# PEER layer on one core: used experts found by VectorE from their products, the spare branch laid out the other way, zeros in one pass

## The chip, the cores and the metric

The kernel runs on one core of one Trainium2 chip. The metric is device time in microseconds (us) for one whole execution; the figure of a kernel is the median of several runs. One execution of the kernel before was also profiled, and all rows below are read from that profile. PE is the matmul engine, DVE the vector engine, ACT the scalar engine, POOL the GpSimd engine and SP the queue that issues most plain DMAs. PE's weight loads have a row of their own, PEld; the rows of an engine's sequencer (branches, waits) carry a q behind the name, as in PEldq.

## The reference, cut to what matters

One decoder layer on 256 tokens of width 2048: attention, then a product-key expert layer (PEER), then a gated embedding, each followed by a layer norm. The change lies in the expert layer. Each token picks 8 x 16 = 128 of 16384 experts, and each expert is one row of `u` and one row of `v`:

```
ub = u[eb]; vbk = v[eb]
act = gelu(einsum('the d,td->the', ub, xb))
w = gb * act
out = einsum('the,thed->td', w, vbk)
```

`eb` holds the expert numbers and `gb` the softmax gates. An expert number is `ia * 128 + ib`.

## The kernel before, in words

**Two ways for tokens.** The first 88 tokens (`NSP`) are done sparsely: POOL gathers their `u` and `v` rows into buffers `gb`, and DVE multiplies and sums them (L854, L864). For the other 168 tokens (`NDT`) the kernel computes all experts by matmul. The sparse work is spread over the dense stages, so many gathers for each dense block.

**Stage u.** `u_block(ia)` multiplies 128 experts of one `ia` with all dense tokens (L210, 32 PE records of 128x168 a block) and writes gelu of it into a table A0, A1 or A2 (one row for each `ib`, one column for each `ia` and token). Their weights `wf<-peer_u` are 1 MB for each block, in 5 buffers.

**Gates.** `gate_work` multiplies the tables with the gates, three tokens (`GB`) at a time. DVE compares with a row of numbers (L937, L939), ACT scales the one-hot rows into a high and a low half (L943, L944), PE multiplies (L951, L952: `ps_G`), and DVE multiplies the table in place (L968). It runs twice: for `ia` 0 to 67 (part 0) beside the u blocks 68 and after, and for `ia` 68 to 127 (part 1) beside the first v blocks. Each run has 56 groups of three tokens. The PE stream of part 0 is placed by the scheduler, the DVE stream by hand (`keep`).

**Counts.** Besides the two gate products there is a third for each token, of the unscaled one-hot rows: it counts how many times an expert was chosen. In part 0 it adds up all tokens in one PSUM bank that is held for it (`ps_cnt`, L954). In part 1 it adds up three tokens (L958) and DVE takes the maximum over groups (L974, L976).

**Lists.** `list_work` turns the counts into a list of used experts: a mask `m` (L1019), ranks by small matmuls, then the index tiles `idxV` and `idxW`. Part 0 lists up to 46 blocks of 128 used experts, part 1 up to 40 (`CAPS`).

**Stage v.** For each of the 86 listed blocks POOL gathers 128 rows of `v` (`vf`, 1 MB, 5 buffers) and of the stored tables (`wc`), and PE multiplies them into six PSUM banks (L1209, 32 records a block). The banks are first zeroed by a matmul (`v_bank`, L1216), with PE weights `ident` and data `zero` in float32.

**The branch.** If more experts are used than the lists hold, 42 more blocks follow (`rest`). This is decided at run time by `tc.If(more > 0)` (L1334), which each engine takes for itself. For this input the list holds all, so the 42 blocks are skipped. Behind the branch PE does the last three blocks (`held`) bank by bank, and then layer norm and the gated embedding.

Of the kernel before, what the change touches and what calls it, by code (L numbers as in the profile page):

```python
# [9 lines left out]
F32 = mybir.dt.float32  # L10
F32R = mybir.dt.float32r
F16 = mybir.dt.float16
U32 = mybir.dt.uint32
AF = mybir.ActivationFunctionType
ALU = mybir.AluOpType
AX = mybir.AxisListType
# [3 lines left out]
P = 128  # L20
T = 256
# [18 lines left out]
SEG1 = 68  # L40
# [3 lines left out]
PARTS = ((0, SEG1), (SEG1, SEG2))  # L44
# [5 lines left out]
NSP = sum(n for _, n in GROUPS)  # L50
# [10 lines left out]
GB = 3  # L61

EARLY, HEARLY = 5, 7
OHB = 4

STAG, LEAD, NWC = 3, 4, 8
NZERO = 3
# [91 lines left out]
def build(tc, a, out):  # L159
# [7 lines left out]
    def pbank(pool, name, tag="bank", bufs=4):  # L167
        return pool.tile([P, 512], F32, name=name, tag=tag, bufs=bufs)
# [450 lines left out]
    gin = pools.open("gin", "left", bufs=1)  # L619
    io128 = gin.tile([P, P], F16, name="io128")  # L620

    zero = gin.tile([P, 1], F32, name="zero")
    nc.gpsimd.memset(zero, 0.0)
    eig, eact, ew = [], [], []
    for i, (_, n) in enumerate(GROUPS):
# [187 lines left out]
    def gathers(n):  # L813

        nonlocal due
        due += n
        while due >= 1:
            due -= 1
            run(sparse, 1)
# [97 lines left out]
        keep(nc.tensor.matmul(ps[:, :nd * P], sel[2], ys[2][:, d0 * P:(d0 + nd) * P],  # L917
                              start=False, stop=False))

    def gate_work(oh, parts, s0, ns, group, counts, listed):  # L920

        def one_hot(t0, n):
            def rows(x, m):
                return x[:, None, :].to_broadcast([P, n, m])

            def cols(x, m):  # L930
                return x[:, t0:t0 + n, None].to_broadcast([P, n, m])

            ohb = oh.tile([P, group, P], F16, name="ohb", tag="ohb", bufs=OHB)
            eq = oh.tile([P, group, ns], F16, name="eq", tag="eq", bufs=OHB)
            hi = oh.tile([P, group, ns], F16, name="hi", tag="hi", bufs=OHB)
            lo = oh.tile([P, group, ns], F16, name="lo", tag="lo", bufs=OHB)
            keep(nc.vector.tensor_tensor(eq[:, :n], rows(io128[:, s0:s0 + ns], ns), cols(iaT, ns),  # L937
                                         op=ALU.is_equal))
            keep(nc.vector.tensor_tensor(ohb[:, :n], rows(io128, P), cols(ibT, P),  # L939
                                         op=ALU.is_equal))  # L940
            for j in range(n):
                t = slice(t0 + j, t0 + j + 1)
                nc.scalar.mul(hi[:, j, :], eq[:, j, :], ghf[:, t])  # L943
                nc.scalar.mul(lo[:, j, :], eq[:, j, :], glf[:, t])  # L944
            return ohb, eq, hi, lo

        def product(t0, n, ohb, eq, hi, lo):
            ps = pbank(pa, "ps_G")
            for j in range(n):
                o = ps[:, j * ns:(j + 1) * ns]  # L950
                nc.tensor.matmul(o, ohb[:, j, :], hi[:, j, :], start=True, stop=False)  # L951
                nc.tensor.matmul(o, ohb[:, j, :], lo[:, j, :], start=False, stop=True)  # L952
                if counts is not None:
                    nc.tensor.matmul(counts, ohb[:, j, :], eq[:, j, :], start=t0 + j == NSP,  # L954
                                     stop=t0 + j == T - 1)
            if counts is None:
                for j in range(n):
                    nc.tensor.matmul(ps[:, n * ns:(n + 1) * ns], ohb[:, j, :], eq[:, j, :],  # L958
                                     start=j == 0, stop=j == n - 1)
            return ps  # L960

        def scale(t0, n, ps):
            g = ps[:, :n * ns].rearrange("p (t a) -> p a t", t=n)
            c0 = 0
            for At in parts:
                dst = At[:, :, t0 - NSP:t0 - NSP + n]
                c1 = c0 + At.shape[1]
                keep(nc.vector.scalar_tensor_tensor(dst, g[:, c0:c1], 1.0 / GSCALE, dst,  # L968
                                                    op0=ALU.mult, op1=ALU.mult))
                c0 = c1  # L970
            if counts is None:
                new = ps[:, n * ns:(n + 1) * ns]
                if t0 == NSP:
                    keep(nc.vector.tensor_copy(total_cnt, new))  # L974
                else:
                    keep(nc.vector.tensor_tensor(total_cnt, total_cnt, new, op=ALU.max))  # L976

        total_cnt = counts
        if counts is None:
            total_cnt = oh.tile([P, ns], F32, name="cnts", tag="used2")  # L980
        made, multiplied = [], None
        for t0 in list(range(NSP, T, group)) + [None] * OHB:
            if t0 is not None:
                n = min(group, T - t0)
                made.append((t0, n, one_hot(t0, n)))
            if multiplied:
                scale(*multiplied)
                multiplied = None
            yield
            if made and (len(made) > OHB - 2 or t0 is None):  # L990
                m = made.pop(0)
                multiplied = (m[0], m[1], product(m[0], m[1], *m[2]))
                yield
        if multiplied:
            scale(*multiplied)
        yield from list_work(oh, parts, s0, ns, total_cnt, listed)

    idxV, idxW, over = [], [], []
    total = gin.tile([P, 1], mybir.dt.int32, name="total")

    def list_work(oh, parts, s0, ns, cnt, listed):


        part = len(idxV)
# [11 lines left out]

        store(2)
        m = oh.tile([P, ns], F16, name="m", tag="m")
        keep(nc.vector.tensor_scalar(m, cnt, 1.0, None, op0=ALU.min))  # L1019
        yield  # L1020
        store(1)

# [160 lines left out]
        return vf, wc  # L1183

    fetched = []
    cnt0 = pbank(pa, "ps_cnt")
    work = gate_work(ohp, (A0, A1), *PARTS[0], GB, cnt0[:, :SEG1], 6)
    for ia in range(SEG1, NIA):
        u_block(ia, W_of(ia))

        made = ia - SEG1
        if made < 38:
            run(work, 3)
        elif ia < NIA - 5:
            run(work, 1)
        elif ia == NIA - 5:
            while not run(work, 1):
                pass
            pools.close("a1p", "a0p")
            wcp = pools.open("wcp", "right", bufs=1)  # L1200
            work = gate_work(ohp, (A2,), *PARTS[1], GB, None, 3)
        if ia >= NIA - 4:
            fetched.append(v_fetch(*order.pop(0), sup, wcp, ("wf", "wc")))
        gathers(GUG if made < 38 else GUL)
# [8 lines left out]
    def v_bank(pool, n):  # L1213

        ps = pbank(pool, "ps_v")
        keep(nc.tensor.matmul(ps[:, :n], ident, zero.to_broadcast([P, n]),  # L1216
                              start=True, stop=False))
        return ps

# [104 lines left out]
    for b in range(LEAD + 1, N1 - STAG):  # L1324
        v_blocks(1, wcq)
        gathers(GV)
        if b == N1 - STAG - 1:
            while not run(sparse, 1):
                pass
# [1 line left out]
    natural_parts(ylp)  # L1331

    fbp = pools.open("fbp", "left", bufs=1)
    with tc.If(more > 0, preferred_fallthrough_block=False):  # L1334
        for i, b in rest:
            block = v_fetch(i, b, fbp, fbp, ("vf", "wc_"))
            for d in range(ND):
                v_mm(d, *block, False)
# [372 lines left out]
```

## Time and profile before

| | us |
|---|---|
| median of 3 runs | 1710.34 |
| lowest and highest run | 1708.72, 1712.31 |
| profiled execution | 1708.22 |
| its span in the trace | 1706.4 |
| PE busy | 1682.3 (99%) |
| DVE busy | 1098.9 (64%) |
| ACT busy | 556.1 (33%) |
| POOL busy | 609.5 (36%) |

The busy time of an engine is the union of its instructions. Matmuls overlap in PE, so their printed durations are longer than what one more of them costs: that is the distance between the starts of one and the next. HBM moved 325 GB/s over the span.

### The profile page before, as it was taken

What the parts mean: (1) busy time and instruction counts of PE and PEld (TensorE: products, weight loads), DVE (VectorE), ACT (ScalarE), POOL (GpSimd) and SP (SyncE); (2) the same over time, 40 slices, a digit from 0 to 9 for tenths busy, and PEclk for the clock granted to TensorE, in tenths of its full rate; (3) what the DMA queues carried; (4) which work ended last, traced back from release to release, by engine and by line L of the source; (5) the groups of instructions that cost most, each with busy time, mean ns of one, the idle gap of its engine ahead of it and who ended that gap; (6) DMA issues with size and microseconds to landing.
All of it is one profiled execution on the core that took longest, in us unless ns stands there. A gap on an engine that the chain in (4) does not pass through costs nothing. (4 is left out here: it accounts for less than half of the span.)

```text
span 1706.4 us, 29275 instructions
## 1 busy us (share of the span) xinstructions
PE 1682.3 (99%) x11258; PEld 1563.7 (92%) x11258; DVE 1098.9 (64%) x2290; ACT 556.1 (33%) x1396; POOL 609.5 (36%) x624
## 2 busy tenths in 40 slices
PE   9999999999999999999999999999999999998998
PEld 7888888888889999999999999999999999998886
DVE  5565489763589779844467765785776943333676
ACT  5677468753111100010044552005553000001452
POOL 0134023103345422722232322137554787673000
PEclk9999999999999999999999999999999999999999
DMA  7544644483998999999999999979999999997571
GB/s 294 195 155 162 234 160 156 156 323 133 338 419 327 390 421 417 419 420 421 421 415 405 371 384 392 422 293 394 392 383 382 418 412 415 401 396 281 187 269 50
DMA packets 97444, 555.63 MB, mean 326 GB/s; under 512 B 13366, under 2 KB 16966, under 8 KB 41846
## 3 DMA queue, kind: packets, MB, share of 16 engines
q0 software_dynamic: 43056, 285.38, 41.7%
q1 hardware_dynamic: 52086, 264.99, 40.3%
q10 hardware_dynamic: 2160, 3.34, 0.6%
q8 instruction: 92, 1.51, 0.3%
q14 instruction: 50, 0.41, 0.1%
HBM read 536.80 MB, written 17.04 MB: 325 GB/s over the span
## 5 line engine op out<-in xcount | busy, mean ns | idle before, releaser
L210 PE MATMUL ps_u<-XF,wf 128*128 128x168 f32 x3936 | 581.3, 308 | 7.5 <-DMA wf<-peer_u 7.1
L210 PEld LDWEIGHTS ps_u<-XF,wf 128*128 128x128 f32 x3936 | 562.5, 190 | 14.1 <-issue 11.8
L1209 PE MATMUL ps_v<-wc,vf 128*128 128x168 f32 x2752 | 414.8, 309 | 5.5 <-issue 5.5
L1209 PEld LDWEIGHTS ps_v<-wc,vf 128*128 128x128 f32 x2752 | 395.9, 191 | 7.3 <-issue 6.8
L120 DVE TENSOR_TENSOR wl<-wf,wh 128x1024 fp32r<-128x1024 f32 (+1 forms) x199 | 212.7, 1092 | 109.8 <-ACT wh L119 108.2
L854 DVE SCALAR_TENSOR_TENSOR gb<-gb,xq 128x2048 f32<-128x2048 f32 x88 | 203.4, 2316 | 99.0 <-DMA gb<-u_rows,eig 99.0
L864 DVE SCALAR_TENSOR_TENSOR y<-gb,ew,y 128x2048 f32<-128x2048 f32 x78 | 183.0, 2346 | 76.4 <-DMA gb<-v_rows,eig 76.3
L119 ACT CAST wh<-wf 128x1024 fp32r<-128x1024 f32 (+1 forms) x199 | 172.0, 892 | 121.0 <-PE ps_v L219 33.0
L1114 ACT ACTIVATE A<-ps_u 128x168 f32<-128x168 f32 x128 | 39.6, 310 | 459.7 <-PE ps_u L210 456.8
L198 PE MATMUL ps_qk<-X,wh 128*128 128x512 f32 x512 | 185.2, 401 | 0.0
L886 POOL DMA_INDIRECT gb<-u_rows,eig x88 | 94.6, 1075 | 246.6 <-DVE gb L854 151.4
L886 POOL DMA_INDIRECT gb<-v_rows,eig x88 | 104.3, 1185 | 132.6 <-DVE y L864 36.4
L200 PE MATMUL ps_qk<-X,wl 128*128 128x256 f32 x512 | 145.7, 285 | 0.0
L943 ACT ACTIVATE hi<-eq,ghf 128x68 f16<-128x68 f16 (+1 forms) x336 | 113.0, 336 | 87.4 <-DVE eq L937 87.3
L1180 POOL DMA_INDIRECT vf<-v_rows,idxV x86 | 107.2, 1246 | 83.9 <-PE ps_G L958 45.1
L1180 POOL DMA_INDIRECT wc<-s_w,idxW x86 | 102.9, 1197 | 40.4 <-issue 24.9
L198 PEld LDWEIGHTS ps_qk<-X,wh 128*128 128x128 f32 x512 | 96.4, 188 | 21.9 <-issue 1.0
L210 PE MATMUL ps_q<-XF,wf 128*128 128x256 f32 x512 | 113.5, 379 | 0.0
L944 ACT ACTIVATE lo<-eq,glf 128x68 f16<-128x68 f16 (+1 forms) x336 | 112.3, 334 | 0.0
L968 DVE SCALAR_TENSOR_TENSOR A<-ps_G,A 128x18 f32<-128x18 f32 (+2 forms) x168 | 46.9, 308 | 100.4 <-PE ps_G L958 44.0
L210 PEld LDWEIGHTS ps_q<-XF,wf 128*128 128x128 f32 x512 | 95.9, 190 | 12.3
L200 PEld LDWEIGHTS ps_qk<-X,wl 128*128 128x128 f32 x512 | 96.3, 188 | 2.5 <-issue 1.3
(309 smaller groups left out, 2127.2 us busy)
## 6 DMA issues: line engine op xcount, KB each, us to landing
wf<-peer_u SPq DMA_DIRECT2D x123, 1024.0 KB
wf<-w_qk SPq DMA_DIRECT2D x64, 512.0 KB
wf<-w_out SPq DMA_DIRECT2D x32, 512.0 KB
wf<-peer_wq SPq DMA_DIRECT2D x16, 1024.0 KB
wf<-ple_gate SPq DMA_DIRECT2D x16, 1024.0 KB
s_w<-A SPq DMA_DIRECT2D x14, 672.0 KB
wf<-w_v SPq DMA_DIRECT2D x16, 512.0 KB
wf<-w_sv SPq DMA_DIRECT2D x15, 512.0 KB
```

The source lines that it names most:

```text
L119: self.order(nc.scalar.copy(wh, src))
L120: self.order(nc.vector.tensor_tensor(wl, src, wh.bitcast(F32), op=ALU.subtract))
L198: nc.tensor.matmul(ps, wh[:, j * P:(j + 1) * P], xt[:, dt, :], start=dt == 0, stop=False)
L200: nc.tensor.matmul(ps[:, :T], wl[:, j * P:(j + 1) * P], xt[:, dt, :T], start=False, stop=dt == ND - 1)
L210: nc.tensor.matmul(ps[:, :T - t0], wf[:, dt * P:(dt + 1) * P], xt[:, dt, t0:], start=dt == 0, stop=dt == ND - 1)
L854: keep(nc.vector.scalar_tensor_tensor(g, g, 1.0, xq[i], op0=ALU.mult, op1=ALU.mult, accum_out=eact[i][:, j:j + 1]))
L864: keep(nc.vector.scalar_tensor_tensor(ys[i], g, ew[i][:, j:j + 1], ys[i], op0=ALU.mult, op1=ALU.add))
L886: keep(nc.gpsimd.indirect_dma_start(out=g, out_offset=None, in_=a[kind], in_offset=bass.IndirectOffsetOnAxis(ap=eig[i][:, 0, j:j + 1], axi ...
L943: nc.scalar.mul(hi[:, j, :], eq[:, j, :], ghf[:, t])
L944: nc.scalar.mul(lo[:, j, :], eq[:, j, :], glf[:, t])
L1180: keep(nc.gpsimd.indirect_dma_start(out=dst, out_offset=None, in_=src, in_offset=bass.IndirectOffsetOnAxis(ap=idx[:, b:b + 1], axis=0)))
L1209: return nc.tensor.matmul(psv[d // 3][:, d % 3 * NDT:(d % 3 + 1) * NDT], vf[:, d * P:(d + 1) * P], wc, start=False, stop=last and (d % 3 = ...
```

## The change

Three things are changed.

**Used experts.** The count products and their PSUM bank are gone. After each 24 tokens (`USED`) that have been scaled, DVE takes the largest absolute value of each expert's scaled products over these 24 tokens (`tensor_reduce` from the table in SBUF, one for A0 and one for A1 in part 0, one for A2 in part 1) and folds it into `greatest` with a maximum. There are 7 such turns in each part. The mask is now `greatest > 0`.

**The branch.** The skipped body now stands next in the program and the short other path behind it (`preferred_fallthrough_block=True`). A hint for PE is asked for two blocks ahead of the branch: it names the branch as likely taken.

**Zeros.** `v_bank` multiplies with `io128` and a `zero` that are both float16.

```diff
+USED = 24
-    zero = gin.tile([P, 1], F32, name="zero")
+    zero = gin.tile([P, 1], F16, name="zero")
...
-                if counts is not None:
-                    nc.tensor.matmul(counts, ohb[:, j, :], eq[:, j, :], start=t0 + j == NSP,
-                                     stop=t0 + j == T - 1)
-            if counts is None:
-                for j in range(n):
-                    nc.tensor.matmul(ps[:, n * ns:(n + 1) * ns], ohb[:, j, :], eq[:, j, :],
-                                     start=j == 0, stop=j == n - 1)
...
-            if counts is None:
-                new = ps[:, n * ns:(n + 1) * ns]
-                if t0 == NSP:
-                    keep(nc.vector.tensor_copy(total_cnt, new))
-                else:
-                    keep(nc.vector.tensor_tensor(total_cnt, total_cnt, new, op=ALU.max))
...
+            end = t0 - NSP + n
+            if end % USED and t0 + n < T:
+                return
+            new = greatest if end <= USED else oh.tile([P, SEG1], F32, name="new", tag="used")
+            c0 = 0
+            for At in parts:
+                c1 = c0 + At.shape[1]
+                keep(nc.vector.tensor_reduce(new[:, c0:c1], At[:, :, (end - 1) // USED * USED:end],
+                                             axis=AX.X, op=ALU.max, apply_absolute_value=True))
+                c0 = c1
+            if end > USED:
+                keep(nc.vector.tensor_tensor(greatest[:, :ns], greatest[:, :ns], new[:, :ns],
+                                             op=ALU.max))
...
-        keep(nc.vector.tensor_scalar(m, cnt, 1.0, None, op0=ALU.min))
+        keep(nc.vector.tensor_scalar(m, most, 0.0, None, op0=ALU.is_gt))
...
-    cnt0 = pbank(pa, "ps_cnt")
-        keep(nc.tensor.matmul(ps[:, :n], ident, zero.to_broadcast([P, n]),
+        keep(nc.tensor.matmul(ps[:, :n], io128, zero.to_broadcast([P, n]),
...
+        if b == N1 - STAG - 2:
+            tc.mark_branch_hint_location("rest", "LikelyTaken", [mybir.EngineType.PE])
...
-    with tc.If(more > 0, preferred_fallthrough_block=False):
+    with tc.If(more > 0, preferred_fallthrough_block=True, label="rest"):
```

In the changed kernel the same lines have other numbers, up to 6 away (L1209 is L1208, L1334 is L1336); the names are the same.

On PE, at the branch, the program before has these rows: the last listed v block, the load of the register, the compare, a jump, the 42 spare blocks (x672), a jump at their end, and the held blocks.

```order
L1209 MATMUL ps_v<-wc,vf 128x168 x672
L1252 TENSOR_LOAD total
L1334 COMPARE_AND_BRANCH
L1334 UNCONDITIONAL_BRANCH
L1209 MATMUL ps_v<-wc,vf 128x168 x672
L1334 UNCONDITIONAL_BRANCH
L1209 MATMUL ps_v<-wc,vf 128x168 x18
```

The changed program has, at the same place on PE:

```order
L1208 MATMUL ps_v<-wc,vf 128x168 x672
L1251 TENSOR_LOAD total
L1336 COMPARE_AND_BRANCH
L1208 MATMUL ps_v<-wc,vf 128x168 x672
L1336 UNCONDITIONAL_BRANCH x2
L1208 MATMUL ps_v<-wc,vf 128x168 x18
```

The compare itself now leaps over the 42 blocks, to the second of the two jumps, which leads to the held blocks right behind it. The short path holds one more thing that the rows don't list, a wait for all of PE's earlier matmuls, ahead of its jump in both programs.

The hint stands elsewhere on PE than the diff asks. These are the first rows of PE's stream in the changed program:

```order
L1703 UNCONDITIONAL_BRANCH
L1703 BRANCH_PREFETCH_HINT
L321 MATMUL ps_zero<-M 128x256 x3
L219 MATMUL ps_v<-wh,X 128x512 x2
L220 MATMUL ps_v<-wl,X 128x512 x2
```

The scheduler moved it to the head of the kernel, ahead of the first matmul, since nothing holds it in its place.

On DVE, in part 0, the stream of the changed program at the end of the second turn of 24 tokens reads as follows (A_5121 and A_4434 are the tables A1 and A0, L938 and L940 the comparisons, L962 the scaling, L856 a sparse dot product):

```order
L938 TENSOR_TENSOR eq<-io_4038,iaT 128x204
L940 TENSOR_TENSOR ohb<-io_4038,ibT 128x384
L962 SCALAR_TENSOR_TENSOR A_4434<-ps_G,A_4434 128x6x3
L962 SCALAR_TENSOR_TENSOR A_5121<-ps_G,A_5121 128x62x3
L973 TENSOR_REDUCE new<-A_4434 128x6
L973 TENSOR_REDUCE new<-A_5121 128x62
L977 TENSOR_TENSOR greatest<-greatest,new 128x68
L856 SCALAR_TENSOR_TENSOR gb,eact_4048<-gb,xq_6754 128x2048
```

Before, the three rows from L973 to L977 were not there; the rest stood in the same order.

## Rows read from the trace of the kernel before

**Rows 1.** Stages: busy us of PE, PEld, DVE, ACT, POOL; granted clock, DMA share, GB/s.

```profile
600.00:870.00 270.00, 266.37 (x1835) 261.34 (x1834) 170.26 (x312) 26.63 (x88) 83.69 (x119) 1.00 1.01 420
870.00:1042.00 172.00, 171.81 (x1573) 169.40 (x1571) 126.73 (x261) 87.65 (x355) 54.30 (x58) 1.00 0.99 389
1165.00:1310.00 145.00, 145.00 (x1391) 142.54 (x1388) 111.31 (x238) 76.87 (x312) 82.69 (x79) 1.00 0.99 390
```

**Rows 2.** Waits of PE: us in total, times, longest.

```profile
PE ps_u L210 <- DMA wf<-peer_u: 7.1, 20, 1.7
PE ps_v L1209 <- issue: 5.5, 2, 5.4
```

**Rows 3.** PE in order of time, one group of part 0: start, us.

```profile
902.97 0.19 PE L951 MATMUL ps_G<-hi,ohb 128*128 128x68 f16 x1
...
903.22 0.20 PE L954 MATMUL ps_cnt<-eq,ohb 128*128 128x68 f16 x1
903.25 0.53 PE L210 MATMUL ps_u<-XF,wf 128*128 128x168 f32 x2
```

**Rows 4.** The same, the count products of a group of part 1.

```profile
1164.94 0.25 PE L958 MATMUL ps_G<-eq,ohb 128*128 128x60 f16 x3
1165.02 2.53 PE L1209 MATMUL ps_v<-wc,vf 128*128 128x168 f32 x16
```

**Rows 5.** Line L954: number, ns least/median/most, first and last start.

```profile
L954 PE MATMUL ps_cnt<-eq,ohb x168: 192/194/198, 871.2 to 1040.9; 128*128 128x68 f16 x168
```

**Rows 6.** PE in order of time, the zeroing (L1216) between stages u and v.

```profile
1155.51 2.88 PE L1216 MATMUL ps_v<-zero,ident 128*128 128x504 f32 x6
1158.23 2.16 PE L1209 MATMUL ps_v<-wc,vf 128*128 128x168 f32 x14
1160.22 2.15 PE L1216 MATMUL ps_v<-zero,ident 128*128 128x504 f32 x6
1162.21 2.73 PE L1209 MATMUL ps_v<-wc,vf 128*128 128x168 f32 x18
```

**Rows 7.** PE in order of time, matmuls of 512 columns with one record each.

```profile
1608.26 0.39 PE L217 MATMUL ps_gate<-wh,X 128*128 128x512 f32 x1
1608.49 0.39 PE L218 MATMUL ps_gate<-wl,X 128*128 128x512 f32 x1
```

**Rows 8.** DVE reductions and count maxima: ns least/median/most, first and last start.

```profile
L719 DVE TENSOR_REDUCE iaN<-eq x8: 404/406/421, 687.0 to 698.7; 128x16 f32<-128x256 f32 x8
L734 DVE TENSOR_REDUCE gs<-gate x2: 266/273/280, 655.3 to 776.8; 128x8 f32<-128x128 f32 x2
L976 DVE TENSOR_TENSOR cnts<-cnts,ps_G x55: 202/208/220, 1168.2 to 1309.2; 128x60 f32<-128x60 f32 x55
```

**Rows 9.** Waits of DVE for the gate products: us in total, times, longest.

```profile
DVE A L968 <- PE ps_cnt L954: 37.1, 20, 3.7
```

**Rows 10.** PE's sequencer at L1334: ns, first and last start.

```profile
L1334 PEldq COMPARE_BRANCH x2: 95/2552/5008, 1561.3 to 1563.6; - x2
L1334 PEldq EVENT_SEMAPHORE x1: 51/51/51, 1563.5 to 1563.5; - x1
```

**Rows 11.** PE in order of time, at the branch and behind it.

```profile
1555.13 8.29 PE L1209 MATMUL ps_v<-wc,vf 128*128 128x168 f32 x57
1568.78 4.95 PE L1209 MATMUL ps_v<-wc,vf 128*128 128x168 f32 x17 [5.37 <-issue]
1573.92 2.98 PE L1209 MATMUL ps_v<-wc,vf 128*128 128x168 f32 x19 [0.18 <-issue]
```

**Rows 12.** Busy us and granted clock around two idle stretches, as in rows 1.

```profile
1082.60:1084.40 1.80, 0.06 (x2) 0.05 (x1) 1.54 (x1) 0.31 (x1) 0.00 (x0) 1.00 1.02 422
1568.70:1573.80 5.10, 4.95 (x17) 4.70 (x17) 0.00 (x0) 0.00 (x0) 0.00 (x0) 0.53 0.50 201
```

**Rows 13.** DMA of PE's instructions, and PE's records, from 1400 to 1525.

```profile
q8 instruction: 7, 0.11, 0.4%
...
1400.00:1525.00 125.00, 125.00 (x879) 125.00 (x878) 41.29 (x18) 0.00 (x0) 91.23 (x75) 1.00 1.01 407
```

More of the change, by code (lines that the diff above doesn't have):

```diff
@@ L918, in natural, with gate_work @@
                               start=False, stop=False))
-    def gate_work(oh, parts, s0, ns, group, counts, listed):
+    def gate_work(oh, parts, s0, ns, group, listed):
         def one_hot(t0, n):
@@ L970, in scale @@
                 c0 = c1
-            if counts is None:
-                new = ps[:, n * ns:(n + 1) * ns]
-                if t0 == NSP:
-                    keep(nc.vector.tensor_copy(total_cnt, new))
-                else:
-                    keep(nc.vector.tensor_tensor(total_cnt, total_cnt, new, op=ALU.max))
-        total_cnt = counts
-        if counts is None:
-            total_cnt = oh.tile([P, ns], F32, name="cnts", tag="used2")
+            end = t0 - NSP + n
[11 more added lines that the diff above has]
+                                             op=ALU.max))
+        greatest = oh.tile([P, SEG1], F32, name="greatest", tag="used2")
         made, multiplied = [], None
@@ L995, in gate_work, with list_work @@
             scale(*multiplied)
-        yield from list_work(oh, parts, s0, ns, total_cnt, listed)
+        yield from list_work(oh, parts, s0, ns, greatest[:, :ns], listed)
     idxV, idxW, over = [], [], []
     total = gin.tile([P, 1], mybir.dt.int32, name="total")
-    def list_work(oh, parts, s0, ns, cnt, listed):
+    def list_work(oh, parts, s0, ns, most, listed):
         part = len(idxV)
@@ L1185, in build @@
     fetched = []
-    cnt0 = pbank(pa, "ps_cnt")
-    work = gate_work(ohp, (A0, A1), *PARTS[0], GB, cnt0[:, :SEG1], 6)
+    work = gate_work(ohp, (A0, A1), *PARTS[0], GB, 6)
     for ia in range(SEG1, NIA):
@@ L1200, in build @@
             wcp = pools.open("wcp", "right", bufs=1)
-            work = gate_work(ohp, (A2,), *PARTS[1], GB, None, 3)
+            work = gate_work(ohp, (A2,), *PARTS[1], GB, 3)
         if ia >= NIA - 4:
```

## The prediction

> **What bounds the kernel now.** I read the stages first, since the share of 99% in the table is a mean over stages with different limits. In the two stages that hold the gate work PE hardly rests: busy 171.81 of 172.00 us in part 0 (870 to 1042) and 145.00 of 145.00 in part 1 (1165 to 1310), at full clock [rows 1]. Just before, from 600 to 870, the other limit shows: PE is busy 266.37 of 270.00 and DMA moves 420 GB/s; this is what DMA can do here, and PE's list of waits has 7.1 us for the weights of stage u [rows 1, 2]. In the gate stages DMA moves only 389 and 390, so there PE sets the pace. The one long wait of PE in the whole kernel is 5.4 us for nothing that the profile names [rows 2], and the order of time puts it at the branch, ahead of the first held block at 1568.78 [rows 11]. So PE's stream is the path, and an edit counts for what it takes from this stream.
>
> **Count products.** In part 0 a group is nine matmuls that start from 902.97 on, and the next u matmul starts at 903.25 [rows 3]: 0.28 / 9 = 31 ns each. Their printed 194 ns overlap. There are 168 of them [rows 5], 56 groups of three: 168 x 31 ns = 5.2 us. In part 1, with as many, the three of a group take from 1164.94 to 1165.02 [rows 4], 0.08 us, or up to 0.09 with the rounding of the two times; 56 x 0.085 = 4.8 us. Together 10.0 us.
>
> **Zeros.** The six matmuls have two records each; they hold PE from 1155.51 to 1158.23 and from 1160.22 to 1162.21 [rows 6], 2.72 + 1.99 = 4.7 us. With float16 I expect one record each. The nearest row is a one-record matmul of 512 columns, with 0.23 us from start to start [rows 7]: five of 504 columns and one of 168 make 1.2 us. Gain 3.5 us; the least is nothing (float16 as slow as before), the most 4.7. I take 3.5, because the row has the same width. The first v blocks then start earlier and need their rows of `v` earlier, but no wait of PE for `vf` stands in its list [rows 2].
>
> **What DVE gets.** A reduction of 256 elements takes 406 ns and one of 128 takes 273 [rows 8], so about 1.04 ns an element. Part 0 has 7 turns of 62 x 24 = 1488 elements (1.69 us), 6 x 24 = 144 (0.29) and, but for the first, a maximum (0.2 by L976): 15 us. Part 1 has 7 of 1440 elements (1.64 us) and 6 maxima, 12.7 us, and loses 56 small ones of 208 ns [rows 8], 11.6 us. So part 0 is the tight one: 126.73 us busy of 172.00 [rows 1] become 142 of about 167. This still fits, and DVE spends 37.1 us of that part waiting for the count products [rows 9], which means that it is ahead of PE. Each turn is a lump of about 2 us on an engine that works in order; the comparisons behind it feed ACT, and ACT feeds the next gate product. No row shows such a lump. Its cost for PE is nothing at the least, and at the most all 14 lumps, 27 us; as DVE is ahead, I take near the low end, 0.6 us. The last reduction of part 0 delays the list by 2 us, but the list goes on by one step for each u block of some 5 us, which hides it.
>
> **DMA.** The bytes stay. In part 0, 389 GB/s x 172 / 166.8 = 401, in part 1 390 x 145 / 140.2 = 403; both are under the 420 that DMA showed [rows 1]. So the gain stays, but the reserve shrinks from 30 to 18 GB/s.
>
> **The branch.** Before, PE's sequencer compares at 1561.3 (95 ns, not taken), waits until PE has finished (1563.5), and then jumps over the 42 blocks at 1563.6; this jump takes 5008 ns [rows 10]. PE ends its work at 1563.42 and starts again at 1568.78. Then come 17 records in 4.95 us, at 290 ns each where two neighbours of the full clock are some 143 ns apart: the clock granted there is 0.53, so half, 1.2 GHz [rows 11, 12]. A second, short wait follows at 1573.9.
>
> *The packet.* PE's instructions come by DMA: seven packets from 1400 to 1525, in which PE ran 879 matmuls and 878 weight loads [rows 13], with one wait for each of 27 blocks 255 instructions for a packet; I take 256. So a jump to a packet that isn't there costs 5.0 us, and I read the wait at 1573.9 as the next packet, asked for when the first had come: 1568.7 + 5.2. It puts the edge 17 matmuls, 17 loads and 3 waits, 37 instructions, behind the target of the jump, which thus stood at place 219 of its packet. The changed stream of PE has 734 instructions less ahead of the branch, as I count them in the two programs: 672 of the 336 count products with their loads, 12 in the zeros, 51 waits, less the hint. The short path is now behind the body. Place 219 becomes 253 for the held blocks (219 - 734 + 3 x 256), and 251 for the short path ahead of them. So, whatever the hint does, only one record of the held blocks is in the first packet, and the second packet is needed at once.
>
> *With the hint at work.* The compare jumps at 1561.3 (all times on the clock of before), 2.1 us before PE is done, to a packet that is there; this asks for the next packet, which comes 5.0 to 5.2 us later, at 1566.5. The 18th record of the held blocks starts 16 records of 143 ns later at full clock, at 1568.8, where it started at 1573.92: 5.1 us gained. At half clock it is 2.8. The idle stretch is some 2.7 us; 1.75 us of idle at 1082.6 left the clock at 1.00 and 5.37 us did not [rows 11, 12]. It is nearer to the first, so I take 5.1.
>
> *With no use of the hint.* The compare waits for the first packet until 1566.3, and the second comes at 1571.5; the 18th record starts at 1573.8 at full clock, or 1576.1 at half. After that idle time half is likelier: 1 us lost (0 to 2.3).
>
> What follows the branch is the work of before in the same order, led by PE, so it shifts as a whole.
>
> **The sum.** 10.0 + 3.5 - 0.6 + 5.1 = 18.0 us. The profiled execution took 1708.22 (span 1706.4 and 1.8 around it) and would take 1690.2. The median of the runs is 2.1 above it, so I expect 1692.3 as median and say 1692.
>
> **The rivals.**
> - *The hint does nothing, at its place.* It runs as PE's first instruction, some 1560 us ahead of its branch, and could be forgotten by then. For it: the trace has no hint at all. Against it: a hint that names its branch can be kept until then. 1710.3 - 12.9 + 1 = 1698.4. The Trainium skill ("Runtime: NRT & Kernel Launch", Instruction fetch mechanics) speaks for this rival: it calls the instruction memory a first-in-first-out store that is refilled in order, from which a target fetched at the start would be gone; it also says that a taken branch out of the window forces a fetch, and the 5008 ns agree with that [rows 10]. By the first rule the time is this rival's.
> - *Both packets are there.* If more than one packet is fetched ahead, PE starts the held blocks at 1563.8 and the 18th record at 1566.3: 7.6 us gained instead of 5.1, 1689.8.
> - *The gate gain goes to waits.* If the lumps on DVE or the smaller DMA reserve hold PE up, most of the 10.0 us comes back as waits of PE for `ps_G`'s inputs or for `wf`; with 8 of it lost, 1700, and without the hint's gain 1706.
> - *Slower.* The hint turns the fetch away from the next packet wherever one is due. Each such miss costs 5.0 us; 12.9 us are gained without the branch, so the third miss decides, and four give 1717. Seven packets in 125 us passed without a wait [rows 13], so misses would be new and visible.
>
> **How the numbers follow.** Hint at work 0.43 (1692, its own range 1689 to 1695), both packets 0.12, hint without use 0.28, gain lost to waits 0.11, slower 0.03, all else about as before 0.03. The runs of before lie 3.6 us apart; 0.2% is 3.4 us, about what can be told from no change. The range from 1688 to 1701 takes in the first three and the lighter part of the fourth, some 0.85. Faster 0.94, within 0.2% 0.03, slower 0.03.
>
> **What the profile of after would show.** Six gate matmuls a group about 30 ns apart in both parts, with no PE waits in these stages beyond tenths; the six zeroing matmuls at 0.21 to 0.23 us; reductions of 1.6 to 1.7 us on DVE. At the branch, one compare of PE that takes either 5 us (no use) or well under 1; one record of the held blocks, then an idle stretch up to the second packet. If the 18th record follows the first without a gap, my count of places is wrong. The prediction fails if PE waits in the gate stages add up to more than 3 us, or if the branch costs more than before.

## The result and the profile after

The changed kernel takes 1693.09 us (median of 4 runs, 1691.35 to 1694.99), beside 1710.76 for the kernel before on the same chip. The ratio is 0.9898 (95% interval from 0.988 to 0.9915), and the medians differ by 17.7 us. The forecast was 1692. The profiled executions differ by 16.9 us (1708.22 to 1691.35). On the chips of the experiments the kernel before took 1711.9 to 1717.5 us, so runs are compared by their ratio to it, and stages by the distance between two starts inside one trace.

**Stages.** The views by stretch of the changed kernel, with the columns of [rows 1] (share and GB/s of DMA last):

```profile
870.00:1037.00 167.00, 167.00 (x1395) 163.92 (x1396) 137.45 (x278) 87.67 (x354) 60.92 (x58) 1.00 0.99 397
1040.00:1100.00 60.00, 55.19 (x397) 54.42 (x396) 33.08 (x99) 3.73 (x12) 9.79 (x16) 1.00 1.01 421
1100.00:1120.00 20.00, 20.00 (x155) 19.82 (x154) 20.00 (x81) 1.25 (x4) 3.41 (x6) 1.00 1.01 416
1120.00:1150.00 30.00, 29.63 (x221) 29.18 (x220) 24.13 (x71) 3.28 (x13) 11.85 (x7) 1.00 0.62 230
1160.00:1300.00 140.00, 140.00 (x1219) 137.54 (x1218) 115.28 (x193) 76.36 (x312) 89.97 (x80) 1.00 1.01 404
1545.00:1565.00 20.00, 19.70 (x141) 19.42 (x140) 10.27 (x19) 6.47 (x13) 1.22 (x1) 1.00 0.67 240
```

PE still sets the pace in both gate stages (167.00 of 167.00 and 140.00 of 140.00), DVE has 30 us to spare in part 0, and DMA went up to 397 and 404 GB/s as forecast. New is what stands behind part 0: from 1040 to 1100 DMA is full, at 421, and PE rests for 4.8 of 60 us. At the branch the granted clock stays at 1.00 (2.4 GHz), where it was 0.53 [rows 12].

**What PE waits for**, largest first (us in total, times, longest), to be held against [rows 2]:

```profile
PE ps_u L212 <- DMA wf<-peer_u: 8.9, 18, 2.2
PE ps_x1T L589 <- ACT XF L538: 1.3, 1, 1.3
PE ps_v L219 <- ACT X L254: 1.2, 1, 1.2
PE ps_zero L321 <- DVE M L318: 1.2, 1, 1.2
PE ps_v L1215 <- ACT A L1114: 1.1, 1, 1.1
PE ps_list L1067 <- DVE blk L1081: 0.6, 2, 0.3
```

The wait of 5.4 us at the branch is gone. The weights of stage u cost 8.9 us instead of 7.1, and two entries are new: the zeroing (L1215) waits for ACT, and the list products wait for DVE.

**Part 0 in order of time**, three of its first pieces of gate products on PE (start, us):

```profile
870.45 0.53 PE L212 MATMUL ps_u<-XF,wf 128*128 128x168 f32 x2
870.82 0.19 PE L953 MATMUL ps_G<-lo,ohb 128*128 128x68 f16 x1
870.85 0.20 PE L952 MATMUL ps_G<-hi,ohb 128*128 128x68 f16 x1
870.88 0.53 PE L212 MATMUL ps_u<-XF,wf 128*128 128x168 f32 x2
871.24 0.19 PE L953 MATMUL ps_G<-lo,ohb 128*128 128x68 f16 x1
```

The products stand 30 ns apart, as expected. But they don't come in whole groups as in [rows 3]: the scheduler put one to three between every two u records. Two u records between pieces take 0.36 us (870.88 to 871.24), where two take 0.285 elsewhere: the first one behind a gate product lasts some 80 ns longer. Each such change from gate products back to u matmuls is called a return here, and the gate products between two returns a piece. I counted 49 returns in part 0 before and 69 now.

**Part 1 and the zeros**, PE in order of time:

```profile
1149.72 2.87 PE L212 MATMUL ps_u<-XF,wf 128*128 128x168 f32 x19
1152.43 0.59 PE L1215 MATMUL ps_v<-zero,io 128*128 128x504 f16 x2
1154.16 0.37 PE L1215 MATMUL ps_v<-zero,io 128*128 128x504 f16 x1 [1.14 <-ACT A L1114]
1154.37 2.73 PE L1208 MATMUL ps_v<-wc,vf 128*128 128x168 f32 x18
1156.93 0.66 PE L1215 MATMUL ps_v<-zero,io 128*128 128x504 f16 x3
1157.43 2.19 PE L1208 MATMUL ps_v<-wc,vf 128*128 128x168 f32 x14
1159.47 0.19 PE L952 MATMUL ps_G<-hi,ohb 128*128 128x60 f16 x1
...
1159.63 0.53 PE L1208 MATMUL ps_v<-wc,vf 128*128 128x168 f32 x2
```

Six records have taken the place of the twelve of [rows 6], some 0.2 us each. In front of the third PE waits 1.14 us until ACT has written gelu of one of the last u blocks and so emptied its PSUM bank. In part 1 the six products of a group come in one piece, 1159.47 to 1159.63; the three count products of [rows 4] are gone without a trace.

**DVE's reductions** (times, busy us, mean ns) last 1.69 and 1.65 us, by the line and shape:

```profile
L973 DVE TENSOR_REDUCE new<-A 128x62 f32<-128x1488 f32 x6 | 10.2, 1693 | 0.0
L973 DVE TENSOR_REDUCE new<-A 128x60 f32<-128x1440 f32 x6 | 9.9, 1653 | 0.2
```

**The branch.** First PE in order of time, then the sequencer's part of the branch's line (ns, start):

```profile
1543.80 10.57 PE L1208 MATMUL ps_v<-wc,vf 128*128 128x168 f32 x73
1554.67 5.37 PE L1208 MATMUL ps_v<-wc,vf 128*128 128x168 f32 x36 [0.30 <-PEq L1336]
```

```profile
L1336 PEldq COMPARE_BRANCH  x1: 408/408/408, 1552.3 to 1552.3; - x1
L1336 PEldq EVENT_SEMAPHORE  x1: 51/51/51, 1554.4 to 1554.4; - x1
```

The jump of 5008 ns [rows 10] has become a taken compare of 408 ns, some 2 us before PE is done. PE goes on after 0.30 us, and all 36 records follow without a gap. The second idle stretch that I had expected behind the first record isn't there.

**Where the time came from.** Distances in us between starts on PE, from the order of time of each trace; "18th" is the 18th record of the held blocks, "end" PE's last record. The lower rows belong to the experiments.

| kernel | u 0 to 72 | u 72 to 105 | u 105 to 127 | u 127 to v 1 | v 1 to 28 | v 28 to 82 | v 82 to 18th | to end |
|---|---|---|---|---|---|---|---|---|
| before | 338.7 | 170.1 | 110.0 | 14.1 | 141.1 | 252.5 | 15.2 | 126.3 |
| after | 337.5 | 166.5 | 111.3 | 11.8 | 136.6 | 253.4 | 7.5 | 126.2 |
| after_again | 339.2 | 166.5 | 111.6 | 11.8 | 136.6 | 253.3 | 7.6 | 126.2 |
| no_hint | 338.9 | 166.5 | 113.0 | 11.9 | 141.1 | 253.9 | 15.4 | 126.2 |
| branch_alone | 338.5 | 170.1 | 110.5 | 14.1 | 145.7 | 252.6 | 7.5 | 126.2 |
| gate_alone | 338.4 | 166.5 | 114.2 | 14.1 | 142.4 | 253.3 | 13.0 | 126.1 |
| zeros_alone | 338.8 | 170.1 | 110.3 | 12.0 | 151.7 | 252.6 | 14.7 | 126.2 |
| pieces | 338.1 | 164.4 | 115.6 | 11.8 | 136.6 | 253.4 | 7.5 | 126.1 |
| pairs | 338.6 | 162.4 | 115.6 | 12.8 | 134.2 | 252.5 | 7.6 | 126.2 |
| lazy | 338.5 | 166.5 | 112.7 | 10.5 | 136.6 | 253.4 | 7.6 | 126.2 |
| late_stores | 339.8 | 166.5 | 105.8 | 11.9 | 139.6 | 253.3 | 7.5 | 126.2 |
| double_reductions | 338.5 | 167.5 | 115.4 | 11.9 | 143.0 | 255.2 | 7.5 | 126.2 |
| best | 339.5 | 162.4 | 109.0 | 10.4 | 144.9 | 253.8 | 8.0 | 126.2 |
| best_again | 338.6 | 162.4 | 108.9 | 11.3 | 142.5 | 252.5 | 7.6 | 126.2 |

After against before: 1.2 ahead of the gates (where the change does nothing; the second run of the changed kernel doesn't have it), 3.6 in part 0, -1.3 behind it, 2.3 at the zeros, 4.5 in part 1, -0.9 between v blocks 28 and 82, 7.7 at the branch, 0.1 at the end: 17.2. Block 0 started 0.4 us later, so the last record comes 16.8 us earlier, as the spans say (1706.4 and 1689.6).

### The profile page after: what moved, and what is told of

It reads as the page before. It is cut to its first block, busy times and chain, and to the rows that moved or that the text cites. A ratio compares the mean times of both kernels' runs of the same rounds, so it can differ in the third digit from the quotient of the medians.

```text
span 1689.6 us, 28494 instructions
## 1 busy us (share of the span) xinstructions
PE 1667.0 (99%) x10916; PEld 1550.4 (92%) x10916; DVE 1117.8 (66%) x2267; ACT 555.7 (33%) x1396; POOL 609.1 (36%) x624
## 5 line engine op out<-in xcount | busy, mean ns | idle before, releaser
L1208 PE MATMUL ps_v<-wc,vf 128*128 128x168 f32 x2752 | 411.9, 308 | 0.3 <-PEq L1336 0.3
L1208 PEld LDWEIGHTS ps_v<-wc,vf 128*128 128x128 f32 x2752 | 393.5, 190 | 2.9 <-issue 2.3
L856 DVE SCALAR_TENSOR_TENSOR gb<-gb,xq 128x2048 f32<-128x2048 f32 x88 | 203.4, 2315 | 99.8 <-DMA gb<-u_rows,eig 99.7
L202 PE MATMUL ps_qk<-X,wl 128*128 128x256 f32 x512 | 145.7, 285 | 0.0
L944 ACT ACTIVATE hi<-eq,ghf 128x68 f16<-128x68 f16 (+1 forms) x336 | 112.7, 336 | 77.8 <-DVE eq L938 67.8
L1180 POOL DMA_INDIRECT wc<-s_w,idxW x86 | 98.1, 1140 | 40.4 <-issue 24.6
L962 DVE SCALAR_TENSOR_TENSOR A<-ps_G,A 128x18 f32<-128x18 f32 (+2 forms) x168 | 46.5, 305 | 73.1 <-PE ps_G L953 66.0
```

The source lines that it names most:

```text
L202: nc.tensor.matmul(ps[:, :T], wl[:, j * P:(j + 1) * P], xt[:, dt, :T], start=False, stop=dt == ND - 1)
L856: keep(nc.vector.scalar_tensor_tensor(g, g, 1.0, xq[i], op0=ALU.mult, op1=ALU.mult, accum_out=eact[i][:, j:j + 1]))
L1180: keep(nc.gpsimd.indirect_dma_start(out=dst, out_offset=None, in_=src, in_offset=bass.IndirectOffsetOnAxis(ap=idx[:, b:b + 1], axis=0)))
L1208: return nc.tensor.matmul(psv[d // 3][:, d % 3 * NDT:(d % 3 + 1) * NDT], vf[:, d * P:(d + 1) * P], wc, start=False, stop=last and (d % 3 = ...
```

## The experiments

Twelve runs, in four lots: the first four on one chip, the next four on a second, the three after them on the first again, the last on a third. In each lot the kernel before ran on the same chip. All ratios are to it, with 95% intervals.

### The parts one by one

**no_hint.** The changed kernel, less

```diff
-            tc.mark_branch_hint_location("rest", "LikelyTaken", [mybir.EngineType.PE])
```

> The changed kernel without the line that asks for the hint; the new layout stays. Theory (the hint does it): the taken compare of PE takes 5.0 us like the jump of before, from about 1552.3 to 1557.3, PE stands idle for about 2.7 us, and the 18th record of the held blocks starts at about 1559.7 or later (1557.16 with the hint): 1695.7, and 1698.4 if a second packet is missing right behind it. A second idle stretch shows where the packet really ends: after one record by the prediction's count of places, after more records if that count is wrong. Rival (the layout alone does it, the hint is without use): the compare takes 0.4 us again, no idle stretch, 1693.1.

Ratio 0.9954 (0.9936 to 0.9971), so of the 17 us some 8 are left; the 7.9 us that the branch takes more (15.4 us for 7.5) account for most of what is gone. In the table this trace also has 4.5 us of unnamed stalls in v blocks 1 to 28 (last section). They need not show in the ratio: the kernel before took 1714.5 and 1717.4 us in its two lots on this chip, where it took 1710.8 and 1711.9 on the chips without such stalls, and no trace of it from this chip was taken. PE in order of time at the branch, and the compare:

```profile
1544.82 18.83 PE L1208 MATMUL ps_v<-wc,vf 128*128 128x168 f32 x131
1565.96 0.38 PE L1208 MATMUL ps_v<-wc,vf 128*128 128x168 f32 x1 [2.30 <-PEq L1333]
1570.39 6.79 PE L1208 MATMUL ps_v<-wc,vf 128*128 128x168 f32 x35 [4.05 <-issue]
```

```profile
L1333 PEldq COMPARE_BRANCH  x1: 4102/4102/4102, 1561.5 to 1561.5; - x1
```

The compare takes 4102 ns, PE idles 2.30 us, does exactly one record, and idles 4.05 us more. So the layout without the hint is worth nothing (15.4 us from block 82 to the 18th record, 15.2 before). And the count of places was right: one record of the held blocks stands in the target's packet. The instruction packets that came in the 16.7 us from the start of the compare on (packets, MB, share), without the hint and then with it:

```profile
q8 instruction: 3, 0.05, 1.1%
```

```profile
q8 instruction: 1, 0.02, 0.4%
```

With the hint two packets fewer follow the branch: the target's and the one behind it were there already. Nor were they fetched shortly ahead of it. From the start of the trace to the compare PE got as many packets without the hint as with it:

```profile
q8 instruction: 81, 1.33, 0.3%
```

```profile
q8 instruction: 81, 1.33, 0.4%
```

The hint with the old layout was not run, so it isn't shown whether the hint needs the new one.

**branch_alone.** The kernel before with the hint and `preferred_fallthrough_block=True, label="rest"`.

> The kernel before with the branch part of the change alone (hint and layout). Theory: the whole 7.7 us of the branch come back here: from the last listed block to the 18th record of the held blocks 7.5 us where it was 15.2, at full clock; 1703.0. Rival (the gain needs the shorter stream, because the place of the target in its packet decides): 5.1 us, with an idle stretch behind the first records of the held blocks; 1705.6.

Ratio 0.9954 (0.9937 to 0.9972). From block 82 to the 18th record 7.5 us, at full clock, with a taken compare of 767 ns: the whole 7.7 us. The rival is out, as far as the time goes. But in this program the target's packet ends some 17 records behind the target, so it could not have shown a gap as clearly as the shorter stream. The packets of the 16.7 us from the compare on are two here, where the kernel before has three over the same time:

```profile
q8 instruction: 2, 0.03, 0.7%
```

So here the hint saved one packet, the target's, and the next one came in time behind the 17 records. `pairs` and `best`, whose streams are of other lengths, have two as well. That both packets are there is thus a finding on the changed kernel, not one on every hinted branch.

**gate_alone.** The changed kernel with the zeros and the branch of before.

> The changed kernel with the branch and the zeros of before, so that only the count products are gone and the reductions are there. Theory (the terms add up): blocks 72 to 105 of stage u gain about 3.6 us, block 1 to block 28 of stage v about 4.5, some 2 us are given back behind them: 1704.3. Rival (part of the 16.8 us belongs to no term, or the parts help each other): more than 1706 or less than 1702.5.

Ratio 0.9919 (0.9901 to 0.9937), 13.9 us less than before by its median, which is more than I had expected; the runs lie from 1701.5 to 1709.6, and the profiled one is the longest. In its trace part 0 gained 3.6 us again, and 4.2 were lost behind it. Part 1 shows 1.3 us more than before, because PE stood still several times in v blocks 1 to 5 for nothing that the profile names (last section). So the stage of part 0 is confirmed. At the branch, which is that of before, 2.2 us less went by (13.0 for 15.2): the jump took 3757 ns, and all 36 records followed without a second wait. The sequencer's branches, then PE in order of time:

```profile
L1333 PEldq COMPARE_BRANCH  x2: 95/1926/3757, 1565.0 to 1567.4; - x2
```

```profile
1571.28 7.04 PE L1208 MATMUL ps_v<-wc,vf 128*128 128x168 f32 x36 [4.11 <-issue]
```

So the cost of the old branch depends on the stream ahead of it, and these 2.2 us belong to two parts at once. By the ratio it would take 1696.5 us where the kernel before takes 1710.3. That is below the 1702.5 of the rival, so this run alone doesn't exclude the rival.

**zeros_alone.** The kernel before with

```diff
+    zero = gin.tile([P, 1], F16, name="zero")
...
+        keep(nc.tensor.matmul(ps[:, :n], io128, zero.to_broadcast([P, n]),
```

> The kernel before with float16 zeros alone. Theory: the zeroing takes 1.2 us instead of 4.7, but PE then waits about 1.1 us for ACT to empty the PSUM bank of one of the last u blocks, as in the changed kernel: last u block to second v block 11.8 us where it was 14.1, 1708.0. Rival (that wait comes from the changed gate work on ACT): no such wait, 10.7 us, 1706.9.

From u block 127 to v block 1 it takes 12.0 us where before took 14.1, with a wait of 1.2 us for ACT: the term and the wait belong to the zeros alone. The whole kernel wasn't faster (ratio 1.0015, 0.9998 to 1.0031): in the profiled execution v blocks 1 to 28 took 151.7 us, 10.6 more than before, in the same unnamed stalls. The gains of the three parts by their ratios (0.0046 for the branch, 0.0081 for the gates, -0.0015 for the zeros) add up to 0.0112, beside 0.0102 and 0.0109 for the whole change. That fits within the intervals, which are some 3 us wide to each side.

### Where part 0's gain went

**after_again** is the changed kernel, as the measure for the three beside it.

> The changed kernel once more, as the measure for the three beside it on this chip: ratio 0.990 to the kernel before, no wait of PE at the branch, 69 pieces of gate products in stage u.

Ratio 0.9891 (0.9875 to 0.9908); the stages repeat within 0.3 us, but for the stretch ahead of the gates.

**pieces.** The order of a group's products turned round, so that the first one needs ACT's last result, and kept in this order:

```diff
-            for j in range(n):
+            for j in reversed(range(n)):
                 o = ps[:, j * ns:(j + 1) * ns]
-                nc.tensor.matmul(o, ohb[:, j, :], hi[:, j, :], start=True, stop=False)
-                nc.tensor.matmul(o, ohb[:, j, :], lo[:, j, :], start=False, stop=True)
+                keep(nc.tensor.matmul(o, ohb[:, j, :], lo[:, j, :], start=True, stop=False))
+                keep(nc.tensor.matmul(o, ohb[:, j, :], hi[:, j, :], start=False, stop=True))
```

> The changed kernel with the gate products of a group in the order in which the last operand comes first, and kept together; nothing else. In stage u they then stand in 46 pieces between the u matmuls where they stood in 69 (49 before the change). Theory: each return from gate products to u matmuls costs about 80 ns (222 ns from the first start to the second where 142.5 is usual), so the 20 more pieces took 1.6 us of the 5.2 that the count products gave in part 0. Then 23 fewer pieces give back 1.9 us in part 0, of which up to 1 us may go to waits for wf behind it: 1691.2 to 1692.2, ratio to before 0.989. Rival (part 0 gave less because reductions on DVE held PE up): the pieces are worth nothing, blocks 72 to 105 take 166.5 us as they did.

Blocks 72 to 105 took 164.4 us instead of 166.5. Of these 2.1 us some 0.5 only moved, since 12 of the 336 products, in two pieces, now stand behind block 105. What all pieces together add to the u records around them fell from 16.03 to 14.35 us: 1.7 us for 23 fewer returns, or 73 ns each, so the returns do cost about what I said. And the kernel wasn't faster (0.9895, 0.9878 to 0.9912): blocks 105 to 127 took 115.6 us instead of 111.6. PE in order of time there, and two stretches behind the wait:

```profile
1070.76 3.16 PE L212 MATMUL ps_u<-XF,wf 128*128 128x168 f32 x21
1077.82 2.46 PE L212 MATMUL ps_u<-XF,wf 128*128 128x168 f32 x10 [3.91 <-DMA wf<-peer_u]
```

```profile
1077.80:1080.30 2.50, 2.48 (x11) 2.50 (x12) 1.20 (x1) 0.00 (x0) 0.00 (x0) 0.65 0.99 413
1080.30:1083.00 2.70, 2.70 (x15) 2.70 (x15) 0.00 (x0) 0.00 (x0) 1.14 (x2) 0.70 1.05 436
```

PE came earlier to weights that came no earlier: its waits for `wf` from 1030 to 1160 are 7.0 us, where `after_again` has 4.0. And the granted clock fell behind the wait of 3.91 us, to a mean of 0.65 and then 0.70, between full (2.4 GHz) and half (1.2 GHz). `after_again` shows the same behind a wait of 2.32 us (0.75, then 0.60), and the first run of the changed kernel, whose longest wait was 2.2 us, doesn't. So part of what is lost behind part 0 can be clock.

**pairs.** Products of two groups at once, in the order of the run before; the loop of `gate_work` then reads:

```diff
+            if i % 2 and made and (len(made) > OHB - 1 or t0 is None):
+                for m in made[:2][::-1]:
+                    multiplied.insert(0, (m[0], m[1], product(m[0], m[1], *m[2])))
+                del made[:2]
...
```

> As the run with fewer pieces, but with the products of two groups one behind the other, in both parts: 28 pieces in stage u and 28 in stage v, 56 where there were 125. Theory of the 80 ns: 41 + 28 returns fewer, 5.6 us, of which some may go to waits for wf: 1687.5 to 1689, ratio 0.987. Rival: four buffers are then full at once, the inputs of the products come late, and PE waits for them; in part 0 every 5 us a wait of tenths would eat it: 1693 or more.

Part 0 took 162.4 us and part 1 134.2, 4.1 and 2.4 less than in the run beside it. Behind part 0 4.0 were lost again, of which some 0.9 are 24 products that moved there, and 1.0 at the zeros, where PE waited 2.3 us for ACT. Ratio 0.9884 (0.9867 to 0.9901), less of a gain than expected and not clear of the changed kernel. PE did not wait for the products' inputs. The sums agree: what a piece adds to the u records around it comes to 19.65 us for before's 504 products in 49 pieces, and to 16.03, 14.35 and 12.72 for 336 in 69, 46 and 28. With 31 ns a product and 80 ns a return that would be 19.5, 15.9, 14.1 and 12.7.

**lazy.** The zeros of the four banks of the u blocks are put off to their first use:

```diff
+                if d % 3 == 0 and len(psv) < 4:
+                    psv.append(v_bank(pp, 3 * NDT))
...
```

> The changed kernel with the zeros of the four banks that held the last u blocks put off: each just ahead of the first v matmul that needs it, the two other banks first. Theory: the third zeroing matmul waited 1.14 us for ACT to empty the bank of a late u block, and this wait goes: from u block 127 to v block 1 10.7 us where it was 11.84; 1692.0. Rival (PE waits at the same bank or for the rows of the first v blocks instead): 11.8 us, or as much lost in the next blocks, 1693.

PE no longer waits for ACT, and 10.5 us stand where 11.8 stood. So of the 1.2 us that the zeros gave less than forecast 1.1 were this wait. In the whole time it can't be seen (0.9892, 0.9875 to 0.9908).

**late_stores.** The stores of part 0's tables begin six u blocks later:

```diff
         def store(n, ia=None):
+            if part == 0 and (ia is None or ia < 18):
+                return
...
```

> The changed kernel, with the nine stores of the part 0 tables (s_w) begun some six u blocks later, on the same queue; nothing else. Theory (what part 0 gains is lost at the weights behind it, because DMA is full there: 418 to 425 GB/s from 1040 to 1115, with the stores among the wf loads, and 230 after 1120): PE's waits for wf between 1070 and 1095 (4.8 us in the first run of the changed kernel, 3.5 in the second) go down by 2 to 4 us, DMA moves more after 1120, and the whole takes 1689 to 1691. Rival (the room behind isn't enough, or the first rows of wc then come late): the waits move to 1100 to 1160, 1693.

The stretches behind part 0, to be held against those of the changed kernel above:

```profile
1040.00:1100.00 60.00, 60.00 (x437) 59.75 (x437) 39.82 (x125) 4.03 (x13) 15.51 (x17) 1.00 1.00 406
1100.00:1120.00 20.00, 20.00 (x155) 19.82 (x154) 19.02 (x75) 1.24 (x4) 3.04 (x4) 1.00 1.01 420
1120.00:1150.00 30.00, 28.48 (x208) 27.57 (x207) 19.21 (x52) 7.26 (x30) 16.02 (x12) 1.00 0.84 330
```

PE is busy 60.00 of 60.00 where it was 55.19, and DMA moves 330 GB/s after 1120 where it moved 230. Blocks 105 to 127 take 105.8 us instead of 111.3. So the wait behind part 0 is DMA's, which has the table stores among the weights there. Whether it is their bytes or their places in the queue ahead of the weights, this run doesn't tell apart. Of the 5.5 us 3.0 are gone again in the unnamed stalls of v blocks 1 to 28. Ratio 0.9875 (0.9845 to 0.9905), not clear of the changed kernel.

**double_reductions.** Every `tensor_reduce` twice, into the same place.

> The changed kernel with every reduction on DVE done twice into the same place, 13 us more of DVE in each part, lumps of 4 us for 2. Theory (the lumps cost PE nothing, the sum of part 0 closes without them: 336 products by 31 ns and 69 returns by 80 ns make 15.9 us, 16.0 is what they take): blocks 72 to 105 take 166.5 us as before, stage v blocks 1 to 28 136.6, 1693. Rival (DVE's lead is nearly used up): PE waits for the inputs of ps_G, up to 1 us a turn, 14 turns, up to 1707.

Part 0 took 167.5 us instead of 166.5, with DVE busy 146.37 of 167.00; in part 1 the unnamed stalls hide what there may be. Ratio 0.9898 (0.9874 to 0.9922). Twice the lumps cost about 1 us in part 0, where the theory had nothing and the rival up to 7. That the lumps of the change cost nothing rests on the sum of part 0, which closes without them.

### A version faster than both

**best** has the pairs, the later stores and the later zeros.

> The changed kernel with the pairs, the later stores and the later zeros together. Theory: the pairs' 5.6 us are no longer lost at wf, the stores give 3, the zeros 1 to 2: 1683 to 1685, ratio to the kernel before 0.984. Rival (stage u's end is set by DMA whatever the order): block 127 of stage u starts no earlier than in the changed kernel (615.3 to 617.3 us behind block 0), and only the 2.3 us of the pairs in stage v and the zeros' 1 are left: 1690.

Ratio 0.9852 (0.9826 to 0.9879). From u block 105 to 127 109.0 us, from 72 to 105 162.4, as the theory has it (block 127 of stage u starts 610.9 us behind block 0, so the rival is out); but v blocks 1 to 28 took 144.9 us, 10.7 more than with the pairs alone, and the whole took 1692.2.

**best_again** is the same kernel.

> The kernel with pairs, later stores and later zeros once more, with more runs. Theory: where PE isn't held up in the first v blocks (the run before lost 8.7 us there in stalls that the profile gives to nothing, as other kernels did on that chip), the ratio to the kernel before is 0.984 and v blocks 0 to 28 take some 140 us. Rival (it is the earlier start of stage v itself that brings the stalls, because the rows of the first blocks come late): v blocks 0 to 28 take 148 to 150 us again and the ratio stays at 0.985 to 0.988.

Ratio 0.9858 (0.9838 to 0.9877), so by the four ratios it beats the changed kernel by some 0.3 to 0.4%, though their intervals just touch. From v 1 to 28 it took 142.5 us, and 148.7 from block 0: the stalls came again, and the 0.984 didn't. These are the rival's figures, but they don't show its cause. Whether the earlier start of stage v brings them isn't settled, since `no_hint` and `zeros_alone`, where stage v starts later, have them too, and `pairs`, on another chip, has none. They go with the chip: all seven kernels traced on the first one have them, and none of the four on the second.

## Why the prediction was right, and where its terms were off

The forecast was 18.0 us, and 17.7 came. The mechanism of each part held, but most sizes were off. That the sum came so near is partly luck. By the stages part 0, part 1 and the zeros gave 5.3 us less than forecast (2.9, 1.2 and 1.2). The branch gave 2.6 more and the lumps cost 0.6 less, and another 1.2 lie ahead of the gates, where nothing was changed.

- **Count products, part 0: 5.2 forecast, 3.6 measured in the stage, 2.3 with what was lost behind it.** "168 x 31 ns" is right for the products. The step that failed is that nothing else on PE would change. Without the third product the scheduler cut the groups up, and 20 more returns to u matmuls at 80 ns gave back 1.6 us. `pieces` shows this by taking 23 returns away. The further 1.3 us were lost behind part 0, where PE waits for `wf`: the rival "the gate gain goes to waits" in small. I had compared DMA's rate inside the gate stages only (401 to 420), not behind them, where DMA was full before too, and the share of [rows 1], 0.99 in both gate stages, left the reserve less sure than the GB/s made it look; `late_stores` shows that the table stores are what fills it.
- **Count products, part 1: 4.8 forecast, 4.5 measured** between blocks 1 and 28; by PE's own records what the gate work adds to the v records around it fell from 18.67 us to 13.95, which is 4.7. In the next blocks 0.9 came back, of which the list of waits names 0.6, the list products that wait for DVE.
- **Zeros: 3.5 forecast, 2.3 measured.** One record each and about 0.2 us, as said. What I left out is ACT: the old 4.7 us had covered its last gelus. `lazy` shows the 1.1 us.
- **DVE's lumps: a loss of 0.6 forecast, nothing seen.** The reductions took 1.69 and 1.65 us, as worked out from [rows 8].
- **The branch: 5.1 forecast, 7.7 measured.** The hint worked from its place at the head of the program. The step that failed is "a packet that is there; this asks for the next packet". The place in the packet was right, which `no_hint` shows with its one record ahead of 4.05 us of idle time; but with the hint the next packet was there as well, as the one packet of `after` for the three of `no_hint` shows. So it went as in the rival "both packets are there", whose 7.6 us fit. The sentence that I had put in the prediction as a test, that a missing gap would mean a wrong count of places, was too narrow: a missing gap could also mean that the second packet had come.
- **The hint without use**, 1 us lost, did not happen, but `no_hint` tells what it would have been: 15.4 us for 15.2, with two idle stretches as the prediction described them.

The Trainium skill ("Runtime: NRT & Kernel Launch", Instruction fetch mechanics) says that a taken branch out of the window forces a fetch; here the jumps of 5008 and 4102 ns without a hint agree. By its first-in-first-out rule the hint's packet would have been gone after 1550 us; the 408 ns of this trace speak against that for a hinted target.

Two things were not settled. Why the packet behind the target was there can't be told from the trace. It was not asked for near the branch, since 81 packets stand ahead of the compare with and without the hint; the first recorded one comes after 25 us, so a fetch at the hint itself isn't seen. And in `branch_alone`, `pairs` and `best` only one packet was saved. Second, the stalls in the first v blocks (below) kept the sum of the parts, each run by itself, from being checked to better than a few us.

## What to carry to other kernels

When work is taken out of a stream that a scheduler places, look at how the rest will be placed: here each return from float16 to float32 matmuls cost some 80 ns, and a third of the gain in part 0 went there. A stage that gains hands its gain on to the next limit, so read the stage behind it too, DMA's rate above all; and work that looks like pure cost (the slow zeros) may have covered someone else's wait. The jump over many instructions cost two waits here where its target stood at the end of a packet (`no_hint`) and one where the next 36 records followed at once (`gate_alone`); with the hint the stretch from block 82 to the 18th record took 7.5 to 8.0 us in every program.

## What the runs showed of the hardware

- The jump of PE over the 42 blocks took 408 to 1177 ns with a hint (408 in the changed kernel, 767 in `branch_alone`, 1162 in `best`, 1177 in `pairs`) and 3757 to 5008 ns without (`gate_alone`, `no_hint`, the kernel before). The hint was still good some 1550 us after it was given.
- In the runs of the first, third and fourth lot, on two other chips, PE stood still in the middle of a v block, between a weight load and its own matmul. In `best_again`, PE and then its weight loads:

```profile
1158.70 1.45 PE L1211 MATMUL ps_v<-wc,vf 128*128 128x168 f32 x9
1161.49 0.45 PE L1211 MATMUL ps_v<-wc,vf 128*128 128x168 f32 x2 [1.35 <-issue]
1163.62 1.03 PE L1211 MATMUL ps_v<-wc,vf 128*128 128x168 f32 x4 [1.69 <-issue]
```

```profile
1160.09 0.19 PEld L1211 LDWEIGHTS ps_v<-wc,vf 128*128 128x128 f32 x1 [0.20 <-issue]
1161.51 0.19 PEld L1211 LDWEIGHTS ps_v<-wc,vf 128*128 128x128 f32 x1 [1.23 <-issue]
1162.22 0.19 PEld L1211 LDWEIGHTS ps_v<-wc,vf 128*128 128x128 f32 x1 [0.53 <-issue]
1163.64 0.46 PEld L1211 LDWEIGHTS ps_v<-wc,vf 128*128 128x128 f32 x3 [1.23 <-issue]
```

The load at 1160.09 was followed by its matmul only at 1161.49, 1.4 us later, and the one at 1162.22 by the matmul at 1163.62, again 1.4. The profile names no wait there, and the matmuls of a block read what its first ones read, so I see no semaphore or transfer that would explain it. Late instructions don't either: no packet of PE's instructions came from 1155 to 1170. The cause stays open.
